# A two-layer conformer and latent-attention trunk on one core: fourth blocks turned through DRAM, the pairs' steps at other slots, another order of the first loads

## The chip, the cores and the metric

The kernel runs on one core of one Trainium2 chip. The time is device microseconds of that core. Three runs of the kernel before gave 1891.77, 1892.09 and 1892.33 us.

The engines are called as in the profile: PE (TensorE, matmuls), DVE (VectorE), ACT (ScalarE), POOL (GpSimd) and SP (SyncE). Each takes its own instructions strictly in order; they meet through semaphores. DMAs are issued here by SP, ACT and POOL.

## The reference, cut to what matters

Two layers, each on 256 rows of 2048 float32 channels:

```
h     = rmsnorm(x, norm_g)
a, glu, cgate, q_down, kv_down, k_pe, mgate, g_conv, g_mla = split(h @ w_in)
conv  = silu(layernorm(depthwise31(a * sigmoid(glu)))) * silu(cgate)
q, k, v from rmsnorm(q_down) @ w_uq and rmsnorm(kv_down) @ w_ukv   (16 heads of 192 / 128)
mla   = chunk_causal_attention(rope(rmsnorm(q)), rope(rmsnorm(k)), v) * silu(mgate)
y     = sigmoid(g_conv) * (conv @ w_proj_conv) + sigmoid(g_mla) * (mla @ w_proj_mla)
x     = x + y @ w_out
```

## The kernel before

**Matmuls.** Every weight and every activation that is multiplied is split in two parts, `hi` and `lo`, and a product is the sum of three matmuls: hi by hi, hi by the activation's lo, lo by the activation's hi. A weight matrix comes as pieces of two blocks of 128 rows by 512 columns (384 or 320 for a few). For each piece SP loads `raw`, ACT copies it to `hi` (`split_hi`, line 192), DVE subtracts for `lo` (`split_lo`, line 211), and PE runs 12 matmuls, six for each half `t` of the rows. A block is eight such pieces (two for `uq` and `ukv`) that add up in one PSUM pair `acc`.

**Slots.** One piece is one slot. `product` (line 290) issues the copies and subtractions of the pieces ahead (hi three ahead, lo two ahead), then the 12 matmuls, then calls `background` (line 243), which issues the steps that are due. `at_slot(n, f)` (line 224) puts step `f` n slots from now, with a cost for DVE and ACT; what is left of DVE's budget of a slot goes to the taps of the depthwise convolution, which wait in a list called `fill`. A block's results are taken out of PSUM by a step 1 + `evac_at` slots after its last piece began. So the program of each engine is one fixed order, decided when the kernel is built; a step late in it holds up all that stands behind it on the same engine.

**Turning.** What was computed with rows on the partitions must come back with channels on the partitions. `turn` (line 340) does it through DRAM: `park` writes the tile in four DMAs, `fetch` reads it back in one, in another order (both on POOL), DVE transposes 32 by 32 blocks, and `then` splits the result for the next product. The fetch is issued 4 slots after the park and the transpose 8 slots after it (`FETCH_AT`, `TURNED_AT`, line 65). The fourth block (c = 3) of `y` (made by `pconv_evac`, line 1109) and of the next layer's `h` (made by `wout_evac`, line 1123) takes another way in `turn4` (line 1015): PE transposes it with an identity matrix, one slot after it came out of PSUM. Those two blocks are needed last by the product that follows, by its pieces 7 and 8 of 8.

**Attention.** The 16 heads go in eight pairs. One pair's share of the order is 12 slots: two pieces of `uq`, two of `ukv`, eight of `glu` or `cgate`. `attention(b)` (line 667) is called after the `ukv` product of pair b and puts its steps at the slots of lines 67 and 68, so that three pairs are under way together. The steps: the rms factors (`stats`), scaling k and parking q and k in DRAM (`scale_k`, eight DMAs), their fetch (`QK_BACK_AT`, two DMAs), the DVE transposes (`QK_TURN_AT`), splits (`NOPE_AT`, `ROPE_AT`, with the subtractions one slot later), the score matmuls, the maxima (`MAX_AT`, tile `nb`), the exponentials on ACT and the parking of the probabilities `pr` (`EXP_AT`, four DMAs), their fetch (`P_BACK_AT`), transpose and split, the product with the values and the copy of the output. As the 12 slots repeat, step n of pair b meets step n + 12 of pair b - 1; of steps due in one slot, those of the earlier pair are issued first.

**The start.** ACT and SP issue the first loads (lines 415 to 427); PE multiplies zeros (`N_WARM`, line 433) until the first real operands are there. Only the first weight piece is split by halves.

In the profile all instructions carry line L127, that of the helper that records the order of issue, so they are told apart by tile names: `s` are scores, `nb` the maxima, `pr` the probabilities, `qk` a pair's queries and keys, `qk_t` their splits, `su` and `u_t` the glu product before and after its turn, `v_t` and `tap` the convolution, `turn_d` the DRAM tiles, `turned` what came back, `gate` and `xres` the tiles that hold a block of y or of x, `tp` PE's transposes.

Of the kernel before, what the change touches and what calls it, by code (L numbers as in the profile page):

```python
# [11 lines left out]

F32 = mybir.dt.float32
F32R = mybir.dt.float32r
# [6 lines left out]
P = 128  # L21
T = 2
# [33 lines left out]
R_QA, R_KVA, R_QR, R_KR, R_N = 0, LORA, 2 * LORA, 2 * LORA + ROPE, 2 * LORA + 2 * ROPE  # L56

KS = 2
N_WARM = 8

# [1 line left out]
EVAC_AT = 1  # L64
FETCH_AT, TURNED_AT = 4, 8

STATS_AT, SCALE_AT, QK_BACK_AT, QK_TURN_AT, NOPE_AT, ROPE_AT, SCORES_AT = 2, 3, 6, 11, 12, 14, 17
MAX_AT, EXP_AT, P_BACK_AT, P_TURN_AT, P_SPLIT_AT, VALUES_AT, O_AT = 18, 19, 23, 28, 30, 32, 34

REVOLUTION_PIECES = 6  # L70

# [44 lines left out]
def trunk(ctx: ExitStack, tc: tile.TileContext, xT, x, g_in, pos, win, wuq, wukv, wpc, wpm, wo, cst, rows, invf, out):  # L116
# [75 lines left out]
    def split_hi(i):  # L192
        if i >= len(pieces) or i in highs:
            return
        load(i)
        highs[i] = split_p.tile([P, KS, pieces[i][1]], F32R, tag="hi", name=f"hi{i}", bufs=4)
        for a in range(0, KS, 1 if i == 0 else KS):
            k = slice(a, a + 1 if i == 0 else KS)

            for step in ("w", "h") if i == a == 0 else ("h", "w"):  # L200
                if step == "w":
                    act.copy(highs[i][:, k], loaded[i][:, k])
                    if i == 0:
                        split_lo(0, k)
                elif i * KS < NCT:
                    for c in range(i * KS + k.start, i * KS + k.stop):
                        first_h(c)
        for a in range(1, LOAD_AHEAD + 1):
            load(i + a)
# [68 lines left out]
    def order_of_products(i, last):  # L278

        two = range(2)
        if i == 0:
            return [(t, kk, p) for kk in range(KS) for p in ((0, 1, 2) if kk else (0, 2, 1)) for t in range(T)]
        high, low = (lambda t, p: [(t, kk, p) for kk in range(KS)]), (lambda t: [(t, kk, 2) for kk in range(KS)])
        if last:
            return high(0, 0) + high(0, 1) + high(1, 0) + low(0) + high(1, 1) + low(1)
        return [e for t in two for p in two for e in high(t, p)] + low(0) + low(1)
# [31 lines left out]
        return lambda k, t: (hi[:, k, t * P : (t + 1) * P], lo[:, k, t * P : (t + 1) * P])  # L320


    def park(src, n, home):
        d = home.tile([4, 32, 4, n // 4], F32, tag=f"t{n}", name="turn_d")
        for i in range(4):
            gps.dma_start(
                d[:, :, i, :].rearrange("j s e -> s j e"),
                src[32 * i : 32 * i + 32, :].rearrange("s (j e) -> s j e", j=4),
            )
        return d  # L330
# [6 lines left out]
        fetch(d, z.rearrange("p i c s -> p (i c s)"))  # L337
        return z

    def turn(src, n, use, dst=None, costs=(0.65, 0.0), then=None, then_costs=(0.0, 0.0), at=TURNED_AT, home=None):  # L340

        d, back = park(src, n, turn_d), []

        def returned():
            if home is None:
                back.append(fetched(d, n))
            else:  # L350
                fetch(d, home)
                back.append(home.rearrange("p (i c s) -> p i c s", i=4, s=32))

        at_slot(FETCH_AT, returned)

        def blockwise():
            z = back[0]
            vec.transpose(z if dst is None else dst.rearrange("p c (i s) -> p i c s", i=4), z)
            z = z.rearrange("p i c s -> p c i s")
            if use:  # L360
                use(z)
            if then:
                at_slot(1, lambda: then(z), *then_costs)

        at_slot(at, blockwise, *costs)
# [26 lines left out]
        rsqrt(out_ap, ms)  # L392


    ident = const.tile([P, P], F32, name="ident")
    make_identity(nc, ident)
    ones = const.tile([P, P], F32, name="ones")
    vec.memset(ones, 1.0 / D)

# [16 lines left out]
    act.dma_start(gx, g_in)  # L416
    load_x(act, 1, 2)
    act.copy(sin2[:, 0, 0, :], ones[:, :HALF])
    for i in range(3):
        load(i)  # L420
    load_x(act, 2, 4)
    load_x(act, 4, 6)
    load_x(sp, 6, 8)
    load(3)
    load_x(sp, 8, 12)
# [1 line left out]
    load_x(sp, 12, 16)  # L427


    zeros = work.tile([P, 512], F32R, tag="junk", name="zeros")  # L430
    vec.memset(zeros.bitcast(F32), 0.0)
    warm = tp_p.tile([P, 512], F32, tag="tp", name="warm")
    for i in range(N_WARM):
        pe.matmul(warm, zeros[:, :P], zeros, start=i == 0, stop=i == N_WARM - 1)

# [79 lines left out]
    for l in range(DEPTH):  # L515
# [496 lines left out]

        def turn4(src, c, use, *costs):


            if c < 3:
                return turn(src, 512, None, then=use, then_costs=costs)
            tps = []  # L1020

            def on_tensor():
                tps.append(tp_p.tile([P, 4, 4, 32], F32, tag="tp", name="tp4"))
                for j in range(4):
                    pe.transpose(tps[0][:, j].rearrange("p i s -> p (i s)"), src[:, j * P : (j + 1) * P], ident)

            at_slot(1, on_tensor)
            at_slot(2, lambda: use(tps[0]), *costs)

        def four(evac_src, dst_hi, dst_lo, c, t):  # L1030

            sl = (slice(None), slice(4 * c, 4 * c + 4), slice(t * P, (t + 1) * P))
            hi, lo = blocks(dst_hi[sl]), blocks(dst_lo[sl])

            def use(z):
                act.copy(hi, z)
                late.append(lambda: vec.tensor_sub(lo, z, hi.bitcast(F32)))

            turn4(evac_src, c, use, 0.65, 0.65)

        def mgate_evac(c, t, ps, keep=keep, A=A):
            g = wide_p.tile([P, 4, P], F32, tag="w", name="gate")
# [80 lines left out]
        def wout_evac(c, t, ps, keep=keep, l=l, last_layer=last_layer):  # L1123
            xt = keep.pop(("x", c, t))
            if last_layer:

                for a, engine in ((0, gps), (256, gps)) if c < 3 else ((0, sp), (256, act)):
                    s = slice(a, a + 256)
                    vec.tensor_add(xt[:, s], ps[:, s], xt[:, s])
                    engine.dma_start(out[t, :, c * 512 + a : c * 512 + a + 256], xt[:, s])  # L1130
                return
            vec.tensor_add(xt, ps, xt)
            gps.dma_start(x1_dram[t, :, c * 512 : (c + 1) * 512], xt)
            if c == 0 and t == 0:
                keep["h"] = [big.tile([P, NCT, SEQ], F32R, tag="big", name=f"hT{i}") for i in range(2)]
            junk = work.tile([P, 512], F32, tag="junk", name="junk")
            late.append(lambda: act.activation(junk, xt, AF.Square, accum_out=ss_x[:, t, c : c + 1]))

            def use(z):
                cts = slice(4 * c, 4 * c + 4)  # L1140
                hi, lo = (blocks(a[:, cts, t * P : (t + 1) * P]) for a in keep["h"])
                for j in range(4):
                    ct = 4 * c + j
                    g = gains[:, (l + 1) * NCT + ct : (l + 1) * NCT + ct + 1]
                    act.activation(hi[:, j], z[:, j], AF.Copy, scale=g)
                    vec.scalar_tensor_tensor(
                        lo[:, j], z[:, j], g, hi[:, j].bitcast(F32), op0=ALU.mult, op1=ALU.subtract
                    )

            turn4(xt, c, use, 1.15, 1.3)  # L1150


        def before_pconv(j, keep=keep):
# [8 lines left out]
        for kind, i, pl in planned:  # L1162
            if kind == "glu":
                at = EVAC_AT
                if i == 0 and l == 0:
                    at = 6
                    for n, (t, c) in enumerate([(0, 0), (0, 2), (1, 0), (1, 2)]):
                        begin, end = first_sums(t, c)
                        at_slot((4, 5, 6, 9)[n], begin)
                        at_slot((9, 9, 10, 12)[n], end, 0.0, 1.5)  # L1170
                    at_slot(13, sum_x, 2.2)
                elif i == 0:
                    at_slot(5, sum_x, 2.2)
                if i == 0:
                    at_slot(10, load_consts)
                product(pl, uses_h, lambda t, ps, i=i: glu_evac(i, t, ps), at, (0.9, 2.2))
# [22 lines left out]
            elif kind == "pmla":  # L1199
                product(pl, stat_of(*keep["o"]), lambda t, ps, i=i: pmla_evac(i, t, ps), costs=(1.25, 0.0))  # L1200
            elif kind == "gconv":
                product(pl, uses_h, lambda t, ps, i=i: gconv_evac(i, t, ps), costs=(0.0, 3.9))
            elif kind == "cgate":
                product(pl, uses_h, lambda t, ps, i=i: cgate_evac(i, t, ps), costs=(0.0, 2.0))
            elif kind == "pconv":
                while "yc" not in keep:
                    run_fill()
                product(pl, stat_of(*keep["yc"]), lambda t, ps, i=i: pconv_evac(i, t, ps), costs=(2.4, 0.0),
                        before=before_pconv if i == 0 else None)
            else:  # L1210
                wout_begin(i)
                last = last_layer and i == 3
                product(pl, stat_of(*keep["y"]), lambda t, ps, i=i, f=wout_evac: f(i, t, ps),
                        0 if last else EVAC_AT, (1.25, 1.5))
        if not last_layer:
            h_hi, h_lo = keep["h"]

# [34 lines left out]
def _rows():  # L1252

    one = np.arange(512).reshape(4, 4, 32).transpose(1, 0, 2).reshape(-1)
    return np.concatenate([512 * b + (one if b < 3 else np.arange(512)) for b in range(4)])


def _layout(inp):
# [62 lines left out]
```

## Time and profile before

| | |
|---|---|
| median of 3 runs | 1892.09 us |
| the profiled execution's own time | 1891.51 us |
| its span, first to last instruction | 1889.7 us |
| PE busy | 1881.9 us, 100% |
| PE weight loads busy | 1589.4 us, 84% |
| DVE busy | 1601.2 us, 85% |
| ACT busy | 1331.5 us, 70% |
| POOL busy | 392.9 us, 21% |
| granted clock of PE | 1.000 |
| DMA | 234 GB/s over the span |

The busy time of PE is that of pipelined matmuls, whose ends are modelled, so 100% does not say that PE never waits: what it loses is seen from the distance of matmul starts and from the chain that ended last. Times in the timeline count from the first instruction; a row is start, duration, engine, operation, output from inputs, shape and count, with the idle time before it and what ended that in brackets.

### The profile page before, as it was taken

How to read it: one execution, taken by the hardware profiler on the slowest of the kernel's cores; microseconds unless marked ns; L12 is line 12 of the kernel's file. 1: busy time of each engine (PE TensorE's matmuls, PEld its weight loads, DVE VectorE, ACT ScalarE, POOL GpSimd, SP SyncE). 2: the span in 40 equal slices, each digit the busy share in tenths (PEclk: the TensorE clock that was granted, in tenths of full speed). 3: DMA queues.
4: the chain of work that ended last, by engine and by line, in shares of the span. 5: the costliest groups of instructions: out<-in, count | busy, mean ns of one | idle time of the engine just before them, and what ended most of it. 6: DMA issues, size and time to landing. Idle time of an engine off the chain costs nothing.

```text
span 1889.7 us, 27378 instructions
## 1 busy us (share of the span) xinstructions
PE 1881.9 (100%) x8744; PEld 1589.4 (84%) x8744; DVE 1601.2 (85%) x2623; ACT 1331.5 (70%) x2350; POOL 392.9 (21%) x734
## 2 busy tenths in 40 slices
PE   9999999999999999999999999999999999999999
PEld 8988888888888888888899888888888888888887
DVE  6899998899999998765679898888999999985654
ACT  7677878878787866544557688688887878474442
POOL 1043433332200000121211443343322000001200
PEclk9999999999999999999999999999999999999999
DMA  9678778776765566677866877787767555666764
GB/s 321 218 251 275 258 236 272 256 256 225 229 210 192 187 218 217 216 236 258 281 209 216 263 263 243 260 266 241 257 228 237 199 189 195 225 213 215 237 224 164
DMA packets 137232, 441.91 MB, mean 234 GB/s; under 512 B 23296, under 2 KB 27136, under 8 KB 137088
## 3 DMA queue, kind: packets, MB, share of 16 engines
q1 hardware_dynamic: 104256, 358.84, 56.5%
q0 software_dynamic: 31968, 80.26, 13.4%
q8 instruction: 68, 1.11, 0.2%
q10 hardware_dynamic: 864, 1.07, 0.2%
q14 instruction: 76, 0.62, 0.1%
HBM read 397.61 MB, written 42.47 MB: 233 GB/s over the span
## 4 chain that ended last, share of the span: by engine, by line
PE 97%; DVE 2%; ACT 1%; DMA 0%; issue 0%; POOL 0%; ACTq 0%; DVEq 0%
PE acc L127 94%; PE s L127 2%; PE o_ps L127 1%; DVE lo L127 1%; DVE v_t L127 0%; DMA x_in<-in_xT 0%; ACT hi L127 0%; ACT tap L127 0%; DVE qk L127 0%; DMA turn_d<-pr 0%; PE tp L127 0%; ACT qk L127 0%; DVE rsq_t L127 0%; DVE ym L127 0%; ACT junk L127 0%
## 5 line engine op out<-in xcount | busy, mean ns | idle before, releaser
L127 ACT CAST hi<-raw 128x1024 fp32r<-128x1024 f32 (+3 forms) x689 | 699.5, 1022 | 411.7 <-PE acc L127 351.7
L127 DVE TENSOR_TENSOR lo<-raw,hi 128x1024 fp32r<-128x1024 f32 (+3 forms) x689 | 811.4, 1181 | 207.8 <-PE acc L127 164.7
L127 PE MATMUL acc<-hi,hT 128*128 128x512 f32 (+2 forms) x1728 | 419.8, 382 | 0.0
L127 PEld LDWEIGHTS acc<-hi,hT 128*128 128x128 f32 x1728 | 319.8, 188 | 59.1
L127 ACT ACTIVATE tap<-u_t,cst 128x256 f32<-128x256 f32 x598 | 260.9, 500 | 14.6 <-DVE v_t L127 13.6
L127 PE MATMUL acc<-hi,h_hi 128*128 128x512 f32 (+2 forms) x864 | 261.3, 384 | 1.1 <-ACT hi L127 1.1
L127 PE MATMUL acc<-hi,h_lo 128*128 128x512 f32 (+2 forms) x864 | 260.1, 382 | 0.0
L127 PE MATMUL acc<-lo,h_hi 128*128 128x512 f32 (+2 forms) x864 | 229.8, 382 | 0.0
L127 PE MATMUL acc<-lo,hT 128*128 128x512 f32 (+2 forms) x864 | 229.3, 382 | 0.0
L127 DVE TENSOR_TENSOR v_t<-v_t,tap 128x512 f32<-128x512 f32 x299 | 205.3, 687 | 10.1
L127 PEld LDWEIGHTS acc<-hi,h_lo 128*128 128x128 f32 x864 | 161.2, 188 | 30.2
L127 PEld LDWEIGHTS acc<-hi,h_hi 128*128 128x128 f32 x864 | 160.4, 188 | 31.0 <-ACT hi L127 1.5
L127 PEld LDWEIGHTS acc<-lo,h_hi 128*128 128x128 f32 x864 | 160.9, 188 | 30.0
L127 PEld LDWEIGHTS acc<-lo,hT 128*128 128x128 f32 x864 | 160.6, 188 | 29.9
L127 POOL DMA_DIRECT2D turn_d<-gate x176 | 95.6, 551 | 321.5 <-DVE gate L127 278.0
L127 DVE SCALAR_TENSOR_TENSOR v_t<-u_t,cst,v_t 128x256 f32<-128x256 f32 x362 | 155.4, 480 | 3.0
L127 POOL DMA_DIRECT2D turned<-turn_d x82 | 45.9, 560 | 519.6 <-DVE v_t L127 317.3
L127 PE MATMUL acc<-hi,oT 128*128 128x512 f32 x512 | 128.1, 390 | 0.0
L127 PE MATMUL acc<-hi,yT 128*128 128x512 f32 x512 | 128.0, 389 | 0.0
L127 PE MATMUL acc<-hi,ycT 128*128 128x512 f32 x512 | 127.8, 389 | 0.0
L127 PE MATMUL acc<-hi,qkc 128*128 128x512 f32 (+1 forms) x512 | 119.0, 364 | 0.2
L127 PEld LDWEIGHTS acc<-hi,oT 128*128 128x128 f32 x512 | 96.1, 188 | 20.1
(171 smaller groups left out, 2139.8 us busy)
## 6 DMA issues: line engine op xcount, KB each, us to landing
raw<-in_win SPq DMA_DIRECT2D x383, 512.0 KB, 4.2
raw<-in_wpm SPq DMA_DIRECT2D x64, 512.0 KB, 3.2
raw<-in_wpc SPq DMA_DIRECT2D x64, 512.0 KB, 4.0
raw<-in_wo SPq DMA_DIRECT2D x64, 512.0 KB, 4.3
raw<-in_wukv SPq DMA_DIRECT2D x32, 512.0 KB, 5.2
turned<-turn_d POOLq DMA_DIRECT2D x50, 256.0 KB, 4.5
raw<-in_win SPq DMA_DIRECT2D x32, 384.0 KB, 4.4
raw<-in_wuq SPq DMA_DIRECT2D x32, 384.0 KB, 3.0
```

The costliest lines, as they stand in the source:

```text
L127: ins = getattr(self.engine, name)(*a, **k)
```

## The change

The fourth block of y and of h now takes the DRAM way too, with the fetch 2 and the transpose 4 slots after the park, and with the half t = 1 parked by SP instead of POOL; both blocks come out of PSUM one slot earlier. The identity matrix and PE's transposes go. The store of the new x is issued behind the parks, the row factor of the second layer three slots later. Ten of the fourteen slots of a pair's steps move. The first loads come in another order, the second weight piece is split by halves too, and PE's first matmuls are 17 of 256 columns instead of 8 of 512. The rows of the weight matrices are laid out on the host to match.

```diff
-N_WARM = 8
+N_WARM = 17
-STATS_AT, SCALE_AT, QK_BACK_AT, QK_TURN_AT, NOPE_AT, ROPE_AT, SCORES_AT = 2, 3, 6, 11, 12, 14, 17
-MAX_AT, EXP_AT, P_BACK_AT, P_TURN_AT, P_SPLIT_AT, VALUES_AT, O_AT = 18, 19, 23, 28, 30, 32, 34
+STATS_AT, SCALE_AT, QK_BACK_AT, QK_TURN_AT, NOPE_AT, ROPE_AT, SCORES_AT = 3, 5, 8, 11, 12, 15, 18
+MAX_AT, EXP_AT, P_BACK_AT, P_TURN_AT, P_SPLIT_AT, VALUES_AT, O_AT = 19, 20, 24, 29, 30, 32, 35
@@ split_hi
-        for a in range(0, KS, 1 if i == 0 else KS):
-            k = slice(a, a + 1 if i == 0 else KS)
+        singly = i < 2
+        for a in range(0, KS, 1 if singly else KS):
+            k = slice(a, a + 1 if singly else KS)
...
-                    if i == 0:
-                        split_lo(0, k)
+                    if singly:
+                        split_lo(i, k)
@@ order_of_products
-        if i == 0:
-            return [(t, kk, p) for kk in range(KS) for p in ((0, 1, 2) if kk else (0, 2, 1)) for t in range(T)]
+        if i < 2:
+            return [(t, kk, p) for kk in range(KS) for p in ((0, 2, 1) if i == kk == 0 else (0, 1, 2)) for t in range(T)]
@@ park, turn
-    def park(src, n, home):
+    def park(src, n, home, queue=gps):
...
-            gps.dma_start(
+            queue.dma_start(
...
-        d, back = park(src, n, turn_d), []
+        d, back = park(src, n, turn_d, queue), []
...
-        at_slot(FETCH_AT, returned)
+        at_slot(fetch_at, returned)
@@ the start
-    ident = const.tile([P, P], F32, name="ident")
-    make_identity(nc, ident)
+    zeros = work.tile([P, 256], F32R, tag="junk", name="zeros")
+    vec.memset(zeros.bitcast(F32), 0.0)
...
-    for i in range(3):
-        load(i)
+    load(0)
+    load(1)
     load_x(act, 2, 4)
-    load_x(act, 4, 6)
+    load_x(sp, 4, 6)
+    load(2)
     load_x(sp, 6, 8)
@@ turn4
-        def turn4(src, c, use, *costs):
+        def turn4(src, c, t, use, *costs):
             if c < 3:
                 return turn(src, 512, None, then=use, then_costs=costs)
-            tps = []
-            def on_tensor():
-                tps.append(tp_p.tile([P, 4, 4, 32], F32, tag="tp", name="tp4"))
-                for j in range(4):
-                    pe.transpose(tps[0][:, j].rearrange("p i s -> p (i s)"), src[:, j * P : (j + 1) * P], ident)
-            at_slot(1, on_tensor)
-            at_slot(2, lambda: use(tps[0]), *costs)
+            turn(src, 512, None, then=use, then_costs=costs, fetch_at=2, at=4, queue=sp if t else gps)
@@ wout_evac
-            gps.dma_start(x1_dram[t, :, c * 512 : (c + 1) * 512], xt)
+            late.append(lambda: gps.dma_start(x1_dram[t, :, c * 512 : (c + 1) * 512], xt))
@@ glu of the second layer
-                    at_slot(5, sum_x, 2.2)
+                    at_slot(8, sum_x, 2.2)
@@ products
-                product(pl, stat_of(*keep["yc"]), lambda t, ps, i=i: pconv_evac(i, t, ps), costs=(2.4, 0.0),
+                product(pl, stat_of(*keep["yc"]), lambda t, ps, i=i: pconv_evac(i, t, ps), 0 if i == 3 else EVAC_AT, (2.4, 0.0),
...
-                last = last_layer and i == 3
                 product(pl, stat_of(*keep["y"]), lambda t, ps, i=i, f=wout_evac: f(i, t, ps),
-                        0 if last else EVAC_AT, (1.25, 1.5))
+                        0 if i == 3 else EVAC_AT, (1.25, 1.5))
@@ _rows
-    return np.concatenate([512 * b + (one if b < 3 else np.arange(512)) for b in range(4)])
+    return np.concatenate([512 * b + one for b in range(4)])
```

In the built program of the changed kernel, POOL's order for one pair reads: eight parks of `qk`, four parks of `pr` (of the pair before; they wait for ACT), two fetches of `qk`, then the parks of `su`. In the kernel before it reads: eight parks of `qk`, two fetches of `qk`, four parks of `pr`, then the parks of `su`. On DVE, between the transposes of `qk` and the maxima `nb` that follow, the changed program has one subtraction `lo` of a weight piece, one convolution tap (two half instructions; in most pairs of the second layer two taps, four halves) and the subtraction `pv` of the probabilities that the kernel before has outside that stretch; the rest is the same work, in another order.

More of the change, by code (lines that the diff above doesn't have):

```diff
@@ L10 @@
 from concourse._compat import with_exitstack
-from concourse.masks import make_identity
 F32 = mybir.dt.float32
@@ L338, in fetched, with turn @@
         return z
-    def turn(src, n, use, dst=None, costs=(0.65, 0.0), then=None, then_costs=(0.0, 0.0), at=TURNED_AT, home=None):
-        d, back = park(src, n, turn_d), []
+    def turn(src, n, use, dst=None, costs=(0.65, 0.0), then=None, then_costs=(0.0, 0.0), at=TURNED_AT, home=None, fetch_at=FETCH_AT, queue=gps):
+        d, back = park(src, n, turn_d, queue), []
         def returned():
@@ L427, in trunk @@
     load_x(sp, 12, 16)
-    zeros = work.tile([P, 512], F32R, tag="junk", name="zeros")
-    vec.memset(zeros.bitcast(F32), 0.0)
-    warm = tp_p.tile([P, 512], F32, tag="tp", name="warm")
+    warm = tp_p.tile([P, 256], F32, tag="tp", name="warm")
     for i in range(N_WARM):
@@ L1037, in use @@
                 late.append(lambda: vec.tensor_sub(lo, z, hi.bitcast(F32)))
-            turn4(evac_src, c, use, 0.65, 0.65)
+            turn4(evac_src, c, t, use, 0.65, 0.65)
         def mgate_evac(c, t, ps, keep=keep, A=A):
@@ L1148, in use @@
                     )
-            turn4(xt, c, use, 1.15, 1.3)
+            turn4(xt, c, t, use, 1.15, 1.3)
         def before_pconv(j, keep=keep):
```

## The prediction

> **What bounds the kernel now.** I read the page first (busy time and the chain that ended last), then the chain in order of time:
>
> ```profile
> PE 1881.9 (100%) x8744; PEld 1589.4 (84%) x8744; DVE 1601.2 (85%) x2623; ACT 1331.5 (70%) x2350; POOL 392.9 (21%) x734
> PE 97%; DVE 2%; ACT 1%; DMA 0%; issue 0%; POOL 0%; ACTq 0%; DVEq 0%
> ```
>
> ```profile
> 1.73 6.34 DMA x_in<-in_xT
> 8.09 0.91 ACT h_hi L127 x2
> 8.99 0.94 ACT hi L127
> ...
> 359.88 23.24 PE acc L127 x108
> 383.12 1.89 PE s L127 x16
> 385.01 8.19 PE acc L127 x36
> 393.20 1.37 PE o_ps L127 x12
> ...
> 863.04 0.87 PE tp L127 x8
> ...
> 1803.17 0.87 PE tp L127 x8
> ```
>
> PE's stream is nearly gapless, so there is little to win: the start, three groups of transposes `tp`, and small waits. The four rows from 359.88 are one pair's PE work: 34.69 us if nothing is late, in pieces of 8.19 / 3 = 2.73 us. The question is whether the other engines still keep up, above all with the attention pairs. The timeline of pair 3 shows DVE, then ACT, POOL and PE:
>
> ```profile
> 262.78 1.83 DVE L127 STREAM_TRANSPOSE qk<-qk 128x768 f32<-128x768 f32 x2
> 264.54 1.18 DVE L127 TENSOR_TENSOR lo<-raw,hi 128x1024 fp32r<-128x1024 f32 x1
> ...
> 285.01 0.16 DVE L127 TENSOR_TENSOR nb<-nb,rs_p 128x4 f32<-128x4 f32 x1
> 285.10 0.95 DVE L127 TENSOR_TENSOR pv<-pr,pv 128x768 fp32r<-128x768 f32 x1
> 285.96 1.82 DVE L127 TENSOR_TENSOR lo<-raw,hi 128x768 fp32r<-128x768 f32 x2
> ...
> 293.28 0.87 DVE L127 SCALAR_TENSOR_TENSOR su<-acc,rinv_x,su 128x256 f32<-128x256 f32 x2 [1.52 <-ACT su L127]
> 294.07 1.21 DVE L127 TENSOR_TENSOR lo<-raw,hi 128x1024 fp32r<-128x1024 f32 x1
> 295.20 1.67 DVE L127 SCALAR_TENSOR_TENSOR v_t<-u_t,cst,v_t 128x256 f32<-128x256 f32 x4
> 296.79 1.22 DVE L127 TENSOR_TENSOR lo<-raw,hi 128x1024 fp32r<-128x1024 f32 x1
> 297.92 1.83 DVE L127 STREAM_TRANSPOSE qk<-qk 128x768 f32<-128x768 f32 x2
> ```
>
> ```profile
> 286.11 1.28 ACT L127 ACT_TABLE_LOAD   x1 [3.18 <-DVE pv L127]
> ...
> 289.46 1.99 ACT L127 CAST hi<-raw 128x1024 fp32r<-128x1024 f32 x2
> 291.48 1.28 ACT L127 ACT_TABLE_LOAD   x1
> 292.77 0.84 ACT L127 ACTIVATE su<-acc,rinv_x 128x256 f32<-128x256 f32 x2
> ```
>
> ```profile
> 276.49 4.37 POOL L127 DMA_DIRECT2D turn_d<-qk  x8 [9.18 <-DVE qk L127]
> 282.63 0.57 POOL L127 DMA_DIRECT2D qk<-turn_d  x1 [1.77 <-DMA turn_d<-qk]
> ...
> 289.86 2.20 POOL L127 DMA_DIRECT2D turn_d<-pr  x4 [3.88 <-ACT pr L127]
> ```
>
> ```profile
> 268.84 0.84 PE L127 MATMUL acc<-lo,h_hi 128*128 128x512 f32 x3
> ```
>
> Followed through, these rows are a ring: the transposes of `qk` (262.78), 22.4 us of DVE work without a pause to the maxima (`nb`, over at 285.17), the exponentials (ACT, 286.11 to 289.46), the sigmoid `su`, DVE's `su` (293.28) and the next transposes (297.92). One turn took 35.14 us where PE needs 34.69. So DVE and ACT already run level with PE here, and a step that lengthens the ring costs time although DVE is idle for 1.52 us inside it.
>
> **The change part by part.**
>
> *The pairs' steps.* `EXP_AT` goes from 19 to 20 and `QK_BACK_AT` from 6 to 8, and 20 is 12 + 8: the exponentials of one pair and the fetch of the next now share a slot, the exponentials first. In the built order POOL therefore issues the four parks of `pr`, which wait for ACT, ahead of the two fetches of `qk`. Before, the fetch (282.63) had its data long before the transposes. Now a new ring closes, transposes, maxima, exponentials, parks, fetch, transposes:
> - DVE from transposes to maxima: 22.4, plus what the built order puts there: one `lo` (296.79 to 297.92: 1.13), one tap of two halves (a quarter of 1.59 each: 0.8), the `pv` subtraction (285.10 to 285.96: 0.86). 25.2; in most pairs of the second layer two taps, 26.0.
> - Exponentials: 286.11 to 289.46, then 0.40 until POOL starts. The wait for `pv` is gone, since it now stands ahead of the maxima. 3.8.
> - Four parks: 2.2. The fetch behind them, 5.4, and 0.1 for DVE to start:
>
> ```profile
> qk<-turn_d POOLq DMA_DIRECT2D x32, 384.0 KB, 5.4
> turned<-turn_d POOLq DMA_DIRECT2D x50, 256.0 KB, 4.5
> turn_d<-gate POOLq DMA_DIRECT2D x176, 64.0 KB, 3.2
> ```
>
> The sum is 36.7 in the first layer and 37.5 in the second. The old ring grows too: 25.2 to the maxima, 3.4 of table load and exponentials, one `hi` (1.0) instead of two, 1.3 and 0.5 to `su`, 0.8 + 1.1 + 1.5 + 1.1 to the transposes, together 36.0 (36.8). Both are over 34.69. What DVE stands still in front of the transposes holds up `lo`, the rotation, the splits; PE waits for these once their lead is gone, and what PE loses it can't win back, as its stream has no other gap to fill. What is queued behind POOL's wait, the `su` parks, has many slots left. The lead: the first `lo` after the transposes is done at 264.54 + 1.18 = 265.7, and PE takes it at 268.84, 3.1 later. The transposes before stood at:
>
> ```profile
> 158.93 1.83 DVE L127 STREAM_TRANSPOSE qk<-qk 128x768 f32<-128x768 f32 x2
> ...
> 192.38 0.97 DVE L127 STREAM_TRANSPOSE qk<-qk 128x768 f32<-128x768 f32 x1
> ...
> 401.25 0.97 DVE L127 STREAM_TRANSPOSE qk<-qk 128x768 f32<-128x768 f32 x1
> ...
> 1131.05 1.83 DVE L127 STREAM_TRANSPOSE qk<-qk 128x768 f32<-128x768 f32 x2
> ...
> 1340.93 1.83 DVE L127 STREAM_TRANSPOSE qk<-qk 128x768 f32<-128x768 f32 x2
> ```
>
> The first row is pair 0, the others pairs 1 and 7 of each layer: one turn of 33.45, then six of 34.81 and, in the second layer, of 34.98. How late pair 1 comes is not shown, since the first turn has less convolution around it; between nothing and the ring's excess of 36.7 - 33.45 = 3.3 I take 1.5, near the middle (1.0 and 2.4 in the bounds below). Pair 7 is then late by 1.5 + 6 x (36.7 - 34.81) = 12.8, less the lead of 3.1: PE loses 9.7. Second layer: 1.5 + 6 x (37.5 - 34.98) - 3.1 = 13.5. Together +23.2. Lower bound, if the fetch were free: the old ring alone, 1.0 + 6 x 1.19 - 3.1 = 5.0 and 1.0 + 6 x 1.82 - 3.1 = 8.8, so +13.8. Upper bound: the fetch takes 6.3: from 256 to 384 KB a fetch costs 0.9 more by the two rows (4.5 and 5.4), and the parks of `pr` just ahead of it in its queue may cost as much once more: 2.4 + 6 x 2.79 - 3.1 = 16.0 and 2.4 + 6 x 3.42 - 3.1 = 19.8, so +35.8. I take 23.2, since 5.4 is the median of this very transfer in this very stage. A gain from the moved steps alone, the lower end below nothing, is rival 2.
>
> The Trainium skill, in "DMA: Bandwidth & Descriptors", section "Anatomy of one DMA", gives a DMA on POOL's path a time of 2.0 us plus its bytes by 436 GB/s; for these 384 KB that is an estimate of 2.9 us. By it the fetch would not be what binds and the sum would be that of the lower bound. The trace disagrees: the row above says 5.4, with other transfers under way.
>
> *Transposes on PE.* Three groups (863.04 to 1803.17) of 8 go at 0.87: -2.6, and about 0.1 each for PE's way back into the product: -2.9.
>
> *Their replacement.* Blocks 1 and 2 show the DRAM way:
>
> ```profile
> 838.78 2.74 POOL L127 DMA_DIRECT2D turn_d<-gate  x5 [13.17 <-DVE gate L127]
> ...
> 845.21 0.57 POOL L127 DMA_DIRECT2D turned<-turn_d  x1
> 848.83 0.56 POOL L127 DMA_DIRECT2D turned<-turn_d  x1 [3.05 <-DMA turn_d<-gate]
> ```
>
> With two queues I count from the end of the last piece: 1.8 until the second half is out of PSUM, 2.2 of issue for four parks, 3.2 to land, 0.6 and 4.5 for the second fetch, 1.3 of transposes and 1.3 to the splits: 14.9. PE needs the block in pieces 7 and 8, six pieces or 16.4 us later. So it costs nothing, with 1.5 us to spare; from the rows, where fetch to landing spans more under load, the other end is 2 us late at each of three places, 6 us. SP's loads of the next raw pieces stand behind its four parks, which wait for DVE's last sum, and DVE's next `lo` stands behind the transposes, which wait some 2 us for the fetch (the transpose is issued 4 slots, 10.9 us, after the park). Both are taken from leads of two pieces and more. One slot earlier out of PSUM means that DVE waits for PE's last matmuls instead of PE's next piece: nothing, since DVE's list has room in these stages. The store of x and the row factor go to places that nobody waits for: 0.
>
> *The start.* Before, piece 2 began after x landed (8.07), two `h_hi` (0.91) and a whole `hi` (0.94). By halves it is half of each: -0.9, with x landing as before, since the loads ahead of it are the same; then the next `hi` comes in just time, so -0.8 (ends 0 and -1.6, the latter if x landed earlier). The 17 x 256 columns are 6% more than 8 x 512 and start earlier: 0.
>
> **The sum.** 23.2 - 2.9 - 0.8 = +19.5 on the profiled execution's 1891.5 (0.6 below the median of the runs): 1911.
>
> **The rivals.**
> 1. *Only the old ring binds.* The fetch is quick and is there when DVE comes. For it: the 5.4 is a median, and it holds time in which other parks were under way. Against it: it is from the same stage, which stays as busy. By the lower bound: 1891.5 + 13.8 - 3.7 = 1902. The formula of the Trainium skill quoted above would have it so.
> 2. *Neither ring binds: faster.* The work that moved in front of the maxima only takes the place of idle time, because DVE comes early to the transposes and ACT has slack. It decides at a ring of 34.7, 2.0 shorter than I count; then the small waits of the attention stage go too, 6 x (34.81 - 34.69) + 6 x (34.98 - 34.69) = 2.5: 1891.5 - 3.7 - 2.5 = 1885. For it: DVE's idle 1.52 in each turn, and ACT's 3.18. Against it: both idle times lie inside the ring, behind the maxima.
> 3. *The fourth blocks come late as well,* three times 2 us: 1917.
> 4. *Nothing to be measured:* the ring at about 35.2 eats just the gain: 1891.
>
> **How the numbers follow.** What a measurement of this kernel can tell is about 0.2%, 3.8 us. Forecast 0.59, rival 1 0.15, rival 2 0.15, rival 3 0.05, rival 4 0.06. Slower by over 0.2%: 0.79; within: 0.06; faster: 0.15. The likeliest case has its own range of 1902 to 1924; the range 1888 to 1923 takes in rivals 1, 3 and 4 and leaves out rival 2 and the upper end of the bounds, together 0.2.
>
> **What would show it.** Right: the scores of the pairs 36 to 37.5 apart, where the turns above were 34.8 to 35.0; DVE idle some us ahead of the `qk` transposes with the `qk` fetch as releaser; POOL's `qk` fetch right behind the parks of `pr`; PE idle only between pairs 1 and 7 of each layer; no PE wait at pieces 7 and 8 of `wout` and of the second layer's first glu; piece 2 at about 9.1 instead of 9.9. Wrong: transposes without a wait and scores 34.7 apart; or a PE wait for `yT` or `hT`.

## The result and the profile after

The changed kernel took 1917.11 us (median of four runs, 1914.87 to 1919.85), the kernel before 1892.21 in the same session: a ratio of 1.0131, 95% interval 1.0115 to 1.0147. The forecast was 1911 us, in a range of 1888 to 1923. The profiled execution is the 1919.85 us one, with a span of 1917.8.

Three lines of the page of the changed kernel: busy times, the chain that ended last, and the group of matmuls that multiply the normalised `q` and `kv` (`uq` and `ukv`), with its idle time at the end.

```profile
PE 1890.7 (99%) x8729; PEld 1590.8 (83%) x8729; DVE 1605.0 (84%) x2633; ACT 1323.7 (69%) x2345; POOL 402.1 (21%) x750
...
PE 85%; DVE 5%; DMA 3%; issue 3%; ACT 3%; POOL 1%; DVEq 0%; ACTq 0%
...
L126 PE MATMUL acc<-hi,qkc 128*128 128x512 f32 (+1 forms) x512 | 124.4, 376 | 14.5 <-DVE su L126 9.5
```

The same group on the page of the kernel before:

```profile
L127 PE MATMUL acc<-hi,qkc 128*128 128x512 f32 (+1 forms) x512 | 119.0, 364 | 0.2
```

The chain, 97% PE before, now runs for 15% of the span through DVE, ACT, POOL, DMA and issue. PE's waits, in the view of waits for the changed kernel (sum, times, longest, in us):

```profile
PE acc L126 <- DVE su L126: 9.5, 6, 2.6
PE acc L126 <- ACT gate L126: 4.9, 4, 2.2
PE acc L126 <- DVE lo L126: 4.7, 6, 1.5
...
PE acc L126 <- DVE yT L126: 0.6, 1, 0.6
```

`su` and `gate` are the steps that empty the PSUM pair of a glu or cgate block, so most of PE's waiting is for PSUM and not for `lo`. Pair 6 of the first layer shows both rings. First DVE, then POOL, ACT and PE (timelines of the changed kernel; idle time and its releaser in brackets):

```profile
364.87 0.16 DVE L126 TENSOR_TENSOR nb<-nb,rs_p 128x4 f32<-128x4 f32 x1
...
373.04 1.23 DVE L126 TENSOR_TENSOR lo<-raw,hi 128x1024 fp32r<-128x1024 f32 x1 [0.71 <-ACT hi L126]
379.74 0.98 DVE L126 STREAM_TRANSPOSE qk<-qk 128x768 f32<-128x768 f32 x1 [5.48 <-DMA turn_d<-gate]
```

```profile
368.85 2.17 POOL L126 DMA_DIRECT2D turn_d<-pr  x4 [4.13 <-ACT pr L126]
371.01 1.12 POOL L126 DMA_DIRECT2D qk<-turn_d  x2
372.12 1.12 POOL L126 DMA_DIRECT2D turn_d<-gate  x2
```

```profile
369.50 1.28 ACT L126 ACT_TABLE_LOAD   x1
370.80 1.27 ACT L126 ACTIVATE gate<-acc,rinv_x 128x512 f32<-128x512 f32 x2
```

```profile
369.53 0.51 PE L126 MATMUL acc<-lo,qkc 128*128 128x384 f32 x2
371.54 2.11 PE L126 MATMUL acc<-hi,qkc 128*128 128x512 f32 x8 [1.50 <-ACT gate L126]
```

POOL parks `pr` at 368.85, 4 us after the maxima, and only then issues the fetch of `qk` (371.01). DVE has nothing left to do at 374.3 and stands still for 5.48 us; the transposes come 8.7 us after the fetch was issued. On the other side ACT empties the cgate block (370.80) behind the exponentials, and PE, done with `uq` at 370.0, waits 1.50 us for that PSUM pair.

From pair 1 to pair 7 the transposes moved by 37.5 us a turn in both layers (194.16 to 419.29 and 1148.51 to 1373.44, a sixth each), where it was 34.81 and 34.98. In the first layer pairs 5 to 7 are the worst: idle times ahead of the transposes of 2.55, 5.48 and 4.50 us. In these POOL issues the parks of `gate` (64 KB each) right behind the fetch; in the glu pairs before them, parks of `su` (32 KB). Whether these parks lengthen the fetch is not shown by a run: in the second layer, with the same parks, the idle times of pairs 4 to 7 are 3.30, 2.48, 2.77 and 3.01 us. Pair 4 of the first layer, POOL and then DVE:

```profile
296.23 2.17 POOL L126 DMA_DIRECT2D turn_d<-pr  x4 [4.09 <-ACT pr L126]
298.39 1.12 POOL L126 DMA_DIRECT2D qk<-turn_d  x2
```

```profile
303.59 1.85 DVE L126 STREAM_TRANSPOSE qk<-qk 128x768 f32<-128x768 f32 x2 [0.24 <-DMA qk<-turn_d]
```

Here the transposes follow the fetch by 5.2 us and DVE hardly waits. (The releaser named is the transfer that ended last by the profile; the transposes read what the fetch of `qk` brought, also where a park of `gate` is named.)

### The profile page after: what moved, and what is told of

Read it like the earlier page. It is cut to its first block, busy times and chain, and to the rows that moved or that the text cites. A ratio compares the mean times of both kernels' runs of the same rounds, so it can differ in the third digit from the quotient of the medians.

```text
span 1917.8 us, 27334 instructions
## 1 busy us (share of the span) xinstructions
PE 1890.7 (99%) x8729; PEld 1590.8 (83%) x8729; DVE 1605.0 (84%) x2633; ACT 1323.7 (69%) x2345; POOL 402.1 (21%) x750
## 4 chain that ended last, share of the span: by engine, by line
PE 85%; DVE 5%; DMA 3%; issue 3%; ACT 3%; POOL 1%; DVEq 0%; ACTq 0%
PE acc L126 83%; DVE lo L126 2%; DMA qk<-turn_d 2%; PE s L126 1%; DVE v_t L126 1%; PE o_ps L126 1%; ACT hi L126 1%; DVE qk_t L126 1%; POOL turn_d L126 1%; ACT L126 1%; ACT pr L126 0%; DMA turned<-turn_d 0%; ACT tap L126 0%; DMA x_in<-in_xT 0%; DVE rsq_t L126 0%
## 5 line engine op out<-in xcount | busy, mean ns | idle before, releaser
L126 POOL DMA_DIRECT2D turn_d<-gate x184 | 100.4, 552 | 325.7 <-DVE gate L126 276.8
L126 PE MATMUL acc<-hi,qkc 128*128 128x512 f32 (+1 forms) x512 | 124.4, 376 | 14.5 <-DVE su L126 9.5
L126 POOL DMA_DIRECT2D turn_d<-qk x128 | 69.9, 554 | 250.9 <-DVE qk L126 174.5
```

The source lines that it names most:

```text
L126: ins = getattr(self.engine, name)(*a, **k)
```

## The experiments

Two theories stood at first: the recorded one (two rings, the one through the fetch the longer, the one through the evacuation of glu close behind), and that the loss is elsewhere (the fourth blocks, the first loads) or has one cause alone. Medians are given with the ratio to the kernel before in the same session; that kernel took 1891.94 to 1892.56 us in the sessions.

**The old steps in the changed kernel.**

```diff
-STATS_AT, SCALE_AT, QK_BACK_AT, QK_TURN_AT, NOPE_AT, ROPE_AT, SCORES_AT = 3, 5, 8, 11, 12, 15, 18
-MAX_AT, EXP_AT, P_BACK_AT, P_TURN_AT, P_SPLIT_AT, VALUES_AT, O_AT = 19, 20, 24, 29, 30, 32, 35
+STATS_AT, SCALE_AT, QK_BACK_AT, QK_TURN_AT, NOPE_AT, ROPE_AT, SCORES_AT = 2, 3, 6, 11, 12, 14, 17
+MAX_AT, EXP_AT, P_BACK_AT, P_TURN_AT, P_SPLIT_AT, VALUES_AT, O_AT = 18, 19, 23, 28, 30, 32, 34
```

> The changed kernel with the fourteen slots of a pair's steps as they were before; everything else as changed. My theory (all the loss sits in the moved steps): the time falls from 1917 to that of the kernel before, less 2.6 to 2.9 us for PE's three groups of transposes, less 0.2 us at the start, plus about 1 us of PE waits for the last block of y: 1890 us (1888 to 1891.5); no PE wait ahead of the ukv products over 0.4 us. Rival (the fourth blocks through DRAM or the first loads cost as well): 1894 us or more, with PE waits at yT, hT or the first pieces that sum to over 4 us.

1888.35 us, 0.9981 (0.9972 to 0.9990), 3.6 us under before. No wait for `su`, `gate`, `lo` or `yT` is left in PE's list. All of the loss, 28.8 us from 1917.1, sits in the moved steps; the rest of the change is a gain of the size forecast.

**The new steps alone in the kernel before** (the reverse edit).

> The kernel before with only the fourteen new slots. My theory: the same turns of 36 to 39 us as in the changed kernel, PE waits ahead of the ukv products, and 1917 to 1921 us. Rival (the loss needs the parks by SP, the later store or the split of the second weight piece): under 1905 us.

1912.05 us, 1.0109 (1.0095 to 1.0123): slower by 20, with the same waits (8.9 us for `su`, 3.9 for `gate`), so the steps need no help from the rest. But the figure is 5 us under the expectation. In this profile the idle times ahead of the transposes of pairs 5 to 7 are 2.4, 2.8 and 3.0 us, where the changed kernel has up to 5.5.

**The fetch one slot earlier.**

```diff
-STATS_AT, SCALE_AT, QK_BACK_AT, QK_TURN_AT, NOPE_AT, ROPE_AT, SCORES_AT = 3, 5, 8, 11, 12, 15, 18
+STATS_AT, SCALE_AT, QK_BACK_AT, QK_TURN_AT, NOPE_AT, ROPE_AT, SCORES_AT = 3, 5, 7, 11, 12, 15, 18
```

> The changed kernel with QK_BACK_AT 7 instead of 8, so that POOL issues the fetch of qk ahead of the parks of pr; the order on DVE and ACT stays. Theory on record (two rings, the one through the fetch the longer): DVE no longer stands ahead of the transposes, the turns of pairs 5 to 7 fall from 39 to 36 us, the ring through the evacuation of glu stays, and the time is 1902 to 1909 us with PE still waiting 0.5 to 2.5 us ahead of the ukv products. Rival A (the fetch behind the parks is the whole loss): 1888 to 1892 us. Rival B (the fetch binds nothing, the evacuation everything): 1914 to 1918 us.

1899.56 us, 1.0043 (1.0029 to 1.0057). DVE no longer waits ahead of the first of a pair's two transposes (one 0.66 in sixteen; ahead of the second, 0.3 to 2.2 us are left in six pairs, most of them at the ends of a layer), yet ahead of twelve of the sixteen `ukv` products PE's starts are 0.5 to 1.8 us apart (0.17 without a wait), and a turn takes 35.4 and 35.9 us. The fetch behind the parks costs 17.5 us, the other ring 11: both bind.

**The exponentials behind the evacuation.**

```diff
-MAX_AT, EXP_AT, P_BACK_AT, P_TURN_AT, P_SPLIT_AT, VALUES_AT, O_AT = 19, 20, 24, 29, 30, 32, 35
+MAX_AT, EXP_AT, P_BACK_AT, P_TURN_AT, P_SPLIT_AT, VALUES_AT, O_AT = 19, 21, 24, 29, 30, 32, 35
```

> The changed kernel with EXP_AT 21 instead of 20: the exponentials now stand behind the evacuation of glu or cgate on ACT, so the PSUM pair that the ukv product needs no longer waits for the maxima; the fetch of qk, at slot 8, also stands ahead of the parks of pr. Theory formed from the trace after (lateness reaches PE through that PSUM pair, which had 0.15 to 0.65 us of lead already before): both rings are open, PE waits ahead of ukv go, 1888 to 1893 us. Rival (DVE's own late lo and rotations hold PE, as the prediction said): PE waits for lo stay and the time stays over 1900 us.

1897.92 us, 1.0035 (1.0021 to 1.0049). The waits ahead of `ukv` go, as expected, all but one of 0.8 us; but 4.7 us of waits for `lo` come, and the time is far over the expectation. DVE and POOL of pairs 2 and 3 show a third ring, through the scaling of k:

```profile
229.67 0.98 DVE L126 STREAM_TRANSPOSE qk<-qk 128x768 f32<-128x768 f32 x1 [2.13 <-DMA qk<-turn_d]
...
251.31 0.38 DVE L126 TENSOR_TENSOR qk<-qk,r_p 128x256 f32<-128x256 f32 x1
...
266.76 0.98 DVE L126 STREAM_TRANSPOSE qk<-qk 128x768 f32<-128x768 f32 x1 [2.39 <-DMA qk<-turn_d]
```

```profile
252.49 4.37 POOL L126 DMA_DIRECT2D turn_d<-qk  x8 [10.95 <-DVE qk L126]
260.59 0.57 POOL L126 DMA_DIRECT2D qk<-turn_d  x1 [3.73 <-DMA turn_d<-qk]
```

k is scaled 21.6 us after the transposes, parked until 256.9, fetched at 260.6 when the parks have landed, and the next transposes wait for it. So `STATS` and `SCALE`, which the prediction left out of its rings, may matter. This was not followed up by itself.

**Only the fetch behind the parks, in the kernel before.**

```diff
-STATS_AT, SCALE_AT, QK_BACK_AT, QK_TURN_AT, NOPE_AT, ROPE_AT, SCORES_AT = 2, 3, 6, 11, 12, 14, 17
+STATS_AT, SCALE_AT, QK_BACK_AT, QK_TURN_AT, NOPE_AT, ROPE_AT, SCORES_AT = 2, 3, 8, 11, 12, 14, 17
```

> The kernel before with QK_BACK_AT 8 instead of 6, nothing else: POOL now parks pr (waiting for ACT) ahead of the fetches of qk, while DVE's stretch from the transposes to the maxima stays 22.4 us. My theory (the ring through the fetch costs only together with the longer stretch): 26.7 to the end of the exponentials, 0.4, parks 2.2, fetch 5.4 to 6.0, 0.1: a ring of 34.8 to 35.4 us beside turns of 34.8 to 35.0, so 1892 to 1898 us, with DVE idle ahead of the transposes by less than 1 us. Rival (the order on POOL costs by itself what the whole change costs there, 17.5 us): 1905 to 1910 us.

1893.74 us, 1.0009 (0.9999 to 1.0018). With DVE's stretch at 22.4 us the same order on POOL costs 1.5 us, which the interval hardly tells from nothing; the idle ahead of the transposes reaches 2.3 us at its longest, over the 1 us expected, in the cgate pairs again. So the order on POOL by itself is not the loss; beside a longer stretch in front of the maxima it is, as the runs below show.

**Which of the steps lengthen the other ring?** First the late steps and the fetch back, then the first steps and the fetch back:

```diff
-STATS_AT, SCALE_AT, QK_BACK_AT, QK_TURN_AT, NOPE_AT, ROPE_AT, SCORES_AT = 3, 5, 8, 11, 12, 15, 18
-MAX_AT, EXP_AT, P_BACK_AT, P_TURN_AT, P_SPLIT_AT, VALUES_AT, O_AT = 19, 20, 24, 29, 30, 32, 35
+STATS_AT, SCALE_AT, QK_BACK_AT, QK_TURN_AT, NOPE_AT, ROPE_AT, SCORES_AT = 3, 5, 6, 11, 12, 14, 17
+MAX_AT, EXP_AT, P_BACK_AT, P_TURN_AT, P_SPLIT_AT, VALUES_AT, O_AT = 18, 19, 24, 29, 30, 32, 35
```

```diff
-STATS_AT, SCALE_AT, QK_BACK_AT, QK_TURN_AT, NOPE_AT, ROPE_AT, SCORES_AT = 3, 5, 8, 11, 12, 15, 18
+STATS_AT, SCALE_AT, QK_BACK_AT, QK_TURN_AT, NOPE_AT, ROPE_AT, SCORES_AT = 2, 3, 6, 11, 12, 15, 18
```

> The changed kernel with ROPE, SCORES, MAX and EXP at 14, 17, 18 and 19 and QK_BACK at 6, as before; STATS and SCALE stay at the new 3 and 5, and the steps of pr at their new slots. My theory (the 11 us that are left with the fetch at 7 come from the maxima and exponentials, one slot nearer to the evacuation of glu): 1888 to 1890 us, no PE wait over 0.5 us ahead of ukv. Rival (q and k parked two slots later hold up the fetch and the transposes): 1893 us or more, with DVE idle ahead of the transposes.

> The complement: the changed kernel with STATS, SCALE and QK_BACK at 2, 3 and 6 as before; ROPE, SCORES, MAX and EXP stay at the new 15, 18, 19 and 20. My theory: as with the fetch at 7, the ring through the evacuation: turns of 35.4 to 35.9 us, PE waits 0.5 to 1.8 us ahead of ukv, 1898 to 1901 us. Rival (the later parks of q and k make that loss): 1888 to 1892 us.

1904.58 us, 1.0061 (1.0046 to 1.0076), and 1886.74 us, 0.9973 (0.9961 to 0.9984). My theory falls in both: the other steps at their new slots, the maxima and exponentials among them, cost nothing (1.6 us less than the run with all old steps, 1888.35), and the loss hangs on `STATS` and `SCALE`. Why the first of the two is 5 us above the run with the fetch at 7 stays open; PE also waits 4.9 us there for `qk_t`. The second beats the kernel before and the changed one. Its DVE timeline for one turn (pair 3 to pair 4):

```profile
260.88 1.82 DVE L126 STREAM_TRANSPOSE qk<-qk 128x768 f32<-128x768 f32 x2
...
285.13 0.16 DVE L126 TENSOR_TENSOR nb<-nb,rs_p 128x4 f32<-128x4 f32 x1
285.22 0.96 DVE L126 TENSOR_TENSOR lo<-raw,hi 128x768 fp32r<-128x768 f32 x1
286.09 1.48 DVE L126 TENSOR_TENSOR v_t<-v_t,tap 128x512 f32<-128x512 f32 x2
287.76 1.23 DVE L126 TENSOR_TENSOR lo<-raw,hi 128x1024 fp32r<-128x1024 f32 x1 [0.18 <-PE acc L126]
288.90 0.88 DVE L126 SCALAR_TENSOR_TENSOR v_t<-u_t,cst,v_t 128x256 f32<-128x256 f32 x2
291.58 0.88 DVE L126 SCALAR_TENSOR_TENSOR su<-acc,rinv_x,su 128x256 f32<-128x256 f32 x2 [1.80 <-ACT su L126]
292.37 1.22 DVE L126 TENSOR_TENSOR lo<-raw,hi 128x1024 fp32r<-128x1024 f32 x1
293.50 0.87 DVE L126 SCALAR_TENSOR_TENSOR v_t<-u_t,cst,v_t 128x256 f32<-128x256 f32 x2
294.29 1.22 DVE L126 TENSOR_TENSOR lo<-raw,hi 128x1024 fp32r<-128x1024 f32 x1
295.43 1.83 DVE L126 STREAM_TRANSPOSE qk<-qk 128x768 f32<-128x768 f32 x2
```

The same turn with the fetch at 7 and the first steps at 3 and 5:

```profile
263.89 1.83 DVE L126 STREAM_TRANSPOSE qk<-qk 128x768 f32<-128x768 f32 x2
...
272.53 0.88 DVE L126 SCALAR_TENSOR_TENSOR v_t<-u_t,cst,v_t 128x256 f32<-128x256 f32 x2
...
288.64 0.16 DVE L126 TENSOR_TENSOR nb<-nb,rs_p 128x4 f32<-128x4 f32 x1
288.73 2.09 DVE L126 TENSOR_TENSOR lo<-raw,hi 128x768 fp32r<-128x768 f32 x2
290.73 0.69 DVE L126 TENSOR_TENSOR v_t<-v_t,tap 128x512 f32<-128x512 f32 x1
295.08 0.87 DVE L126 SCALAR_TENSOR_TENSOR su<-acc,rinv_x,su 128x256 f32<-128x256 f32 x2 [3.67 <-ACT su L126]
295.88 1.22 DVE L126 TENSOR_TENSOR lo<-raw,hi 128x1024 fp32r<-128x1024 f32 x1
297.01 0.68 DVE L126 TENSOR_TENSOR v_t<-v_t,tap 128x512 f32<-128x512 f32 x1
297.73 0.88 DVE L126 SCALAR_TENSOR_TENSOR v_t<-u_t,cst,v_t 128x256 f32<-128x256 f32 x2
298.53 1.22 DVE L126 TENSOR_TENSOR lo<-raw,hi 128x1024 fp32r<-128x1024 f32 x1
299.66 1.83 DVE L126 STREAM_TRANSPOSE qk<-qk 128x768 f32<-128x768 f32 x2
```

Both turns hold four taps (a tap is two halves of 256 columns with `u_t`, or one addition of 512 columns with `tap`, which ACT has multiplied), and from `nb` to `su` both take 6.4 us, which ACT sets. In the first, three of the four taps fill that wait, and one lies on the ring (293.50). In the second a single one fills it (290.73); one lies ahead of the maxima (272.53) and two behind `su` (297.01, 297.73), all on the ring, while DVE idles 3.67 instead of 1.80. The turns are 34.55 and 35.77 us: 0.5 more in front of the maxima, 0.7 behind `su`. PE needs 34.69.

That is a new theory: the planner puts taps where DVE's budget has room, and with `STATS` and `SCALE` later there is room early in the stretch. The rival is that parking q and k later costs by itself. Two kernels move only the costs that the planner is told, so that the taps change places and the steps do not. (Eight of the taps also go from DVE's two halves to ACT's multiplication, or back; by the mean durations that is 2.2 us of DVE's work in the whole kernel.) The first has QK_BACK at 7 besides:

```diff
-            at_slot(STATS_AT, stats, 2.2)
-            at_slot(SCALE_AT, scale_k, 1.1)
+            at_slot(2, lambda: None, 2.2)
+            at_slot(3, lambda: None, 1.1)
+            at_slot(STATS_AT, stats)
+            at_slot(SCALE_AT, scale_k)
```

> The changed kernel with QK_BACK_AT 7, and the planner told DVE's costs of the rms factors and of the scaling of k at slots 2 and 3, where they stood before; the two steps themselves stay at 3 and 5. So the convolution taps stand among the other work as in the run with the first steps back (each turn the same number of taps: fewer ahead of the maxima and behind the evacuation, more in the wait between). New theory (the late first steps free budget early in the stretch, the planner puts taps there, and these lengthen the ring): turns fall from 35.8 to 34.6 us and the time from 1899.6 to 1887 to 1890 us. Rival (q and k parked two slots later cost by themselves): 1897 to 1901 us.

The reverse:

```diff
-STATS_AT, SCALE_AT, QK_BACK_AT, QK_TURN_AT, NOPE_AT, ROPE_AT, SCORES_AT = 3, 5, 8, 11, 12, 15, 18
+STATS_AT, SCALE_AT, QK_BACK_AT, QK_TURN_AT, NOPE_AT, ROPE_AT, SCORES_AT = 2, 3, 6, 11, 12, 15, 18
...
-            at_slot(STATS_AT, stats, 2.2)
-            at_slot(SCALE_AT, scale_k, 1.1)
+            at_slot(3, lambda: None, 2.2)
+            at_slot(5, lambda: None, 1.1)
+            at_slot(STATS_AT, stats)
+            at_slot(SCALE_AT, scale_k)
```

> The reverse: first steps at 2, 3 and 6 as before, with the planner told their costs at slots 3 and 5, so that the taps stand as in the changed kernel. New theory (tap placement): turns of 35.4 to 35.9 us and 1896 to 1900 us, against 1886.7 without the moved costs. Rival (late parks): 1886 to 1888 us.

1889.18 us, 0.9983 (0.9973 to 0.9992), with turns of 34.61; and 1899.37 us, 1.0032 (1.0019 to 1.0045), with turns of 35.39 and 35.85. Moving the taps alone takes 10 us off the one and puts 12.6 on the other. What is left for the later parks and the fetch at 7 instead of 6 is 2.4 us with the taps in the wait (1889.2 against 1886.7, where the runs of each of the two kernels spread over 5 us) and nothing with the taps on the ring (1899.6 and 1899.4).

**The fetch ring by itself, and both together.** The first has the first steps at 2 and 3 and the fetch at 8; the second is the changed kernel with only the planner's costs moved, by the diff with slots 2 and 3 above.

```diff
-STATS_AT, SCALE_AT, QK_BACK_AT, QK_TURN_AT, NOPE_AT, ROPE_AT, SCORES_AT = 3, 5, 8, 11, 12, 15, 18
+STATS_AT, SCALE_AT, QK_BACK_AT, QK_TURN_AT, NOPE_AT, ROPE_AT, SCORES_AT = 2, 3, 8, 11, 12, 15, 18
```

> The changed kernel with STATS and SCALE at 2 and 3 as before, QK_BACK at the new 8: the only thing that differs from the 1886.7 us run is that POOL issues the fetch of qk behind the parks of pr. Theory on record for the ring through the fetch: 24.4 + 3.8 + 2.2 + 5.4 to 6.0 + 0.1 = 35.9 to 36.5 us a turn, DVE idle ahead of the transposes, 1895 to 1902 us. Rival (this ring needs the late parks of q and k as well): 1887 to 1890 us.

> The changed kernel, all steps and the fetch at their new slots, with only the planner's costs of the first steps at 2 and 3, so that only the taps move. If the two parts add up (about 11 us from the taps, 17.5 from the fetch): 1904 to 1908 us. If the ring through the fetch binds alone whenever it is there: 1912 to 1917 us.

1906.54 us, 1.0074 (1.0057 to 1.0091), 5 over the expectation, and 1909.60, 1.0088 (1.0073 to 1.0103), between the two expectations. The traces of the first kernel and of the 1886.74 us one have the same order on DVE, ACT and SP, and differ on POOL only in the place of the fetches of `qk`: that alone costs 19.8 us. A turn of the first kernel, DVE's transposes and maxima, POOL, and DVE's next transposes:

```profile
264.35 2.05 DVE L126 STREAM_TRANSPOSE qk<-qk 128x768 f32<-128x768 f32 x2 [0.61 <-DMA qk<-turn_d]
...
288.56 0.16 DVE L126 TENSOR_TENSOR nb<-nb,rs_p 128x4 f32<-128x4 f32 x1
```

```profile
292.54 2.18 POOL L126 DMA_DIRECT2D turn_d<-pr  x4 [9.85 <-ACT pr L126]
294.71 1.13 POOL L126 DMA_DIRECT2D qk<-turn_d  x2
```

```profile
300.54 1.90 DVE L126 STREAM_TRANSPOSE qk<-qk 128x768 f32<-128x768 f32 x2 [1.59 <-DMA turn_d<-su]
```

From 264.35 the turn is 24.4 + 3.8 + 2.2 + 5.8 = 36.2: the recorded sum with a shorter stretch. The 24.4 has `lo` and `pv` ahead of the maxima and no tap. Four kernels with `STATS` and `SCALE` at their new slots part the loss of the 1917 us kernel (medians, us):

| | taps as with the old first steps | taps as in the changed kernel |
|---|---|---|
| fetch ahead of the parks (7) | 1889.2 | 1899.6 |
| fetch behind the parks (8) | 1909.6 | 1917.1 |

The fetch costs 20.4 or 17.5, the taps 10.4 or 7.5; they overlap by 2.9.

**The changed kernel once more.**

> The changed kernel itself once more, for its spread and a second profile. If the fetches of 8.6 to 10 us in pairs 6 and 7 of the first layer and the distance of 5 us to the kernel before with the new slots alone are luck of the transfers, the times spread over 1910 to 1920 us and other pairs are late; if they belong to the program, the median is 1916 to 1918 us and the same pairs stand.

1916.91 us (1914.28 to 1917.99), with idle times of 1.95, 4.73 and 4.37 ahead of the transposes of pairs 5 to 7. It belongs to the program. Why the new steps cost 28.8 us here and 20.1 in the kernel before stays open; the layouts of memory and the phases of the transfers differ, and no run parts them.

## Why the prediction was right, and where it was not

**Direction, place and mechanism: right.** The moved steps carry the whole loss, the fetch of `qk` stands right behind the parks of `pr`, DVE waits for it ahead of the transposes, and the ring takes what was added up: 36.2 us by the rows just shown, with 5.8 for the fetch where 5.4 was put. In the changed kernel's first layer the turns into pairs 3 and 4 take 35.8 and 36.2, those into pairs 6 and 7 take 39.4 and 39.5. The estimate of 2.9 us from the Trainium skill, "DMA: Bandwidth & Descriptors", section "Anatomy of one DMA", is not borne out by any run: the median from issue to landing lies between 5.2 and 6.2 us in every profile. The old ring alone, without the fetch, was put at 36.0 and +13.8 us; the run with the fetch at 7 gives turns of 35.8 in the middle pairs, and 1899.6 against 1888.35, +11.2.

**The sum of the rings: 23.2 forecast, 28.8 measured.** Against the kernel with the old steps PE's attention stage, from the first `uq` matmul to the start of pair 7's product with the values, is 13.1 and 15.3 us longer in the changed kernel's profile, 28.4 together. Term by term:
- *The first turn.* 1.5 us late was taken near the middle of its bounds; it is 2.8 in the first layer (36.39 against 33.63) and 2.6 in the second (36.90 against 34.26).
- *The first layer's turn.* 36.7 forecast, 37.5 measured; the cgate pairs' fetches took up to 8.7 us to the transposes. The second layer's 37.5 was right in the mean, of turns between 36.4 and 39.2. With the first turns, pair 7's transposes come 19.2 and 18.1 us later after pair 0's than with the old steps, where 12.8 and 16.6 were forecast.
- *The lead of 3.1 us.* Subtracted twice, 6.2 in all, it was too small in sum, since PE loses 28.4 of these 37.3 us; and it was taken in the wrong place. It was read at `lo`, but PE meets the lateness earlier, at the PSUM pair of the `ukv` product, and there the lead was nil already before. The row below is the `ukv` product of the kernel before; the first half of `su` (293.28 in the prediction's timeline) was over at 293.76, 0.15 us ahead of it, and PE started 0.36 us after the matmul before, where 0.17 is the distance without a wait. What PE does not lose may be in good part DVE's idle ahead of pair 7's transposes (4.50 and 3.01 us), behind which no `ukv` product of the layer comes; no run shows this.

```profile
293.91 2.09 PE L127 MATMUL acc<-hi,qkc 128*128 128x512 f32 x8
```

- *PE's clock.* Not in the sum at all; some 5 of the 28.4 us, see the last section.

**What lengthens the old ring: right by the sum, without its cause.** The built order was read as 22.4 + `lo` + tap + `pv`, 25.2 to the maxima against a measured 24.9 (fetch at 7); 6.2 from there to `su` against 6.3; 4.5 from there to the transposes against 4.6. In this sum `lo` and `pv` ahead of the maxima (2.0) are won back behind them (1.9), so what lengthens this ring is the tap. The prediction did not ask what put it there. The other steps at their new slots shorten the turn from pair 3 to pair 4, from 35.15 with all old steps to 34.55. Rival 2 had this mechanism (moved work takes the place of idle time) and a time of 1885; the kernel with `STATS`, `SCALE` and the fetch at their old slots runs at 1886.7. What lengthens the ring are tap pieces alone, put there because `STATS` and `SCALE` moved, two steps whose move the prediction gave no price. The ring through the fetch is another matter: it does not pass through `su`, wins nothing back there, and carries `lo` and `pv` in full, 24.4 without any tap.

**Transposes gone, their replacement free: nearly right.** The old steps with all the rest gave −3.6 us, where −3.7 was forecast. But PE does wait for `yT`, which the prediction gave as a sign of being wrong: ten of the eleven profiles with that way through DRAM show waits of 0.4 to 1.6 us in sum, so the 1.5 us to spare were none; each wait is under the 2 us a place of rival 3. `hT` is never waited for.

**The start: right.** Piece 2 was forecast at 9.1 instead of 9.9. In the eleven profiles of kernels with the new start it begins at 8.77 to 9.81, at 9.40 on average; in three with the old one at 9.98 to 10.21, 10.11 on average. That is −0.7. The changed kernel's own profile is the latest of them:

```profile
9.81 0.73 PE L126 MATMUL acc<-hi,h_hi 128*128 128x512 f32 x2 [1.02 <-ACT hi L126]
```

## What to carry to other kernels

Before a step is moved, write down every ring that passes through its slot, and look for the lead where PE meets the lateness first; in the changed kernel that was mostly a PSUM pair, not the operand. A planner that fills spare time puts its fillers where the moved step has left room: what counts is whether that room lies on the ring or in its wait. A DMA that is issued behind another one's wait inherits that wait, which costs next to nothing while the ring through it is hardly longer than the work (1.5 us in the kernel before), and most of the excess beyond that (with the old first steps and the fetch at 8, 19.8 us of time for twelve turns that grew by 24.4 in sum).

## What the runs showed that was not expected

Where two neighbouring matmuls of PE start 2.28 us or more apart, those of 512 columns mostly go at 427 ns instead of 227 for a while. The windows of the changed kernel before and behind the longest wait (it ends at 227.44), and behind a wait of 0.84 us, in which the starts are 1.01 us apart:

```profile
222.00:227.30 5.30, 2.83 (x17) 2.51 (x15) 1.64 (x4) 5.27 (x13) 2.96 (x6) 1.00 0.97 355
227.40:231.60 4.20, 4.16 (x11) 3.31 (x12) 4.03 (x6) 4.14 (x15) 2.50 (x6) 0.59 0.92 265
299.30:303.50 4.20, 4.18 (x18) 3.48 (x19) 4.02 (x6) 4.14 (x15) 3.57 (x8) 1.00 0.98 266
```

The columns are the window, its length, the busy times of PE, PEld, DVE, ACT and POOL with counts, PE's granted clock, DMA share and GB/s. The clock was 0.59 in the 4.2 us behind the long wait, and 11 matmuls went through instead of 18. Over all profiles, twelve pairs of neighbouring matmuls start 2.28 to 2.94 us apart; behind nine of them six to eight matmuls go at the half rate, 1.2 to 1.6 us lost each. Of those 1.0 to 2.03 us apart none shows it beyond a single matmul. In the changed kernel's profile four such waits are followed by 26 matmuls at the half rate, 5.2 us on top of the waits themselves. The Trainium skill, "TensorE: Matmul & The Clock Gate", section "HAM oscillation — how this bites in real kernels", gives as the abstract rule no idle gaps of PE over about 3.4 us; the runs here show the clock reduced after shorter ones, nine of the twelve with starts 2.28 to 2.94 us apart.
